# A hybrid diffusion layer on one core: another order for the prologue and for the gates of the mLSTM

## The chip, the cores and the metric

The kernel runs on one core of a Trainium2 chip. The metric is device time in microseconds (us), and a kernel's time is the median of its runs. The engines are TensorE (PE; PEld is its weight load), VectorE (DVE), ScalarE (ACT), GpSimd (POOL) and SyncE (SP). SP issues nearly all transfers, from one queue, in order.

## The reference

One layer over 1024 latent tokens and 256 context tokens, 1024 wide, float32. Cut to the steps that matter:

```
mod = silu(c) @ w_mod + b_mod                  # 6 pieces of 1024: shift, scale, gate, twice
p   = (LN(x) * (1 + scale1) + shift1) @ w_in   # the same for ctx, with silu(c_ctx)
i, f = p_gates[..., :8] + b, log_sigmoid(p_gates[..., 8:] + b)
mix = [HGRN2(p), mLSTM(conv3x3(q, k), v, i, f)]     # both scan forward and backward
x   = LN(alpha * x + gate1 * (readout(mix) @ w_out))
x   = LN(alpha * x + gate2 * PEER(LN(x) * (1 + scale2) + shift2))   # 8 heads, top 16 of 16384 experts
```

The mLSTM needs running sums of `f` and running maxima per chunk of 128 tokens, in both directions.

## The kernel before

A scheduler decides the order of the instructions on every engine when the kernel is built; the program's order is its guide, and an instruction marked `keep_in_program_order` is not moved ahead of what stands before it. Each engine then runs its own list in order, and waits where an input or a buffer isn't ready. A named tile with `bufs=n` is a ring of n buffers, handed out in the order of the program.

Four stages come before PEER.

**Prologue** (`modcols` L89, `inputs_ln` L164). The first 2048 columns of `w_mod` (shift and scale) come in 8 tiles `w` of 1 MB. For each, TensorE multiplies 1536 columns by the two conditioning vectors (L116), and VectorE sums the last 512 (`macc`, L120 and L122). Two context tiles are loaded ahead of them, `wf` (1 MB of `w_in`) amid them, and the eight tiles of x behind them (L159). The result is turned into columns `modc` (L133, L135). Then each group of tokens is normalised, transposed to PSUM, modulated by ScalarE into `xf` (L180), and split into a high half (float16, L181, VectorE) and a low half (bfloat16, L182, VectorE or, for two of eight k, GpSimd): `xmT`. All projections take both halves.

**Gates** (`gates` L237). 16 columns per token are projected (`oa`), transposed to rows of tokens on 64 partitions (L261), made into log sigmoids there (L266 to L270), scanned by VectorE (L280 to L325), and transposed back to columns `gcol` (L331). The columns are used in the mLSTM alone.

**HGRN2** (`hgrn` L342). Values are projected in two halves (`inputs`, L230, 240 matmuls each), then 8 rounds of `one`, whose projections are L222. `modrows` (L669) makes the other 4096 modulation columns meanwhile: 32 tiles `wm` of 512 KB in a ring of its own, two buffers deep, two matmuls each (L686). `Uprep` (L185) is spread through the stage: it loads one of 128 tiles of the expert table (`us`, 512 KB, ring of two in pool `up`), casts it to a high half (ScalarE, L198), subtracts for the low half (GpSimd, L199), and stores both (`Ud`, L202). 96 of the 128 are called before the mLSTM.

**mLSTM** (`mlstm` L508). For each half of q and k, projections go to a padded grid (`pad`, L545), and VectorE runs the 9 taps of the convolution (L553, L555) over 1024 elements per partition, and after it the chunk states. Readout, output projection and PEER follow.

Of the kernel before, what the change touches and what calls it, by code (L numbers as in the profile page):

```python
# [17 lines left out]
D = 1024  # L18
LAT = 1024
CTX = 256  # L20
# [68 lines left out]
def modcols(g, I, mp, lp):  # L89
# [16 lines left out]
    ps = [g.pp.tile([128, 512], F32, name=n, bufs=2 if n == "pj" else 1) for n in ("pj", "pj", "sc")]  # L106
    acc = mp.tile([128, 2, 512], F32, name="macc")
    xs = inputs_load(g, I, lp, 0, 2)
    g.w0 = []
    for k in range(KD):  # L110
        if k == KD // 2:
            g.w0.append(W(g, I, HI))
        wt = mp.tile([128, 2048], F32, name="w0", bufs=8)
        nc.sync.dma_start(wt, I["w_mod"][0, k * 128:(k + 1) * 128, 0:2048])
        for b in range(3):
            nc.tensor.matmul(ps[b][0:2], g.cs[:, k::8], wt[:, b * 512:(b + 1) * 512], start=(k == 0), stop=(k == KD - 1))  # L116
        for j in range(2):
            c = g.cs[:, 8 * j + k:8 * j + k + 1]
            if k == 0:
                nc.vector.tensor_scalar(acc[:, j], wt[:, 1536:], c, None, op0=OP.mult)  # L120
            else:
                nc.vector.scalar_tensor_tensor(acc[:, j], wt[:, 1536:], c, acc[:, j], op0=OP.mult, op1=OP.add)  # L122
    xs += inputs_load(g, I, lp, 2, NT)
    mr = mp.tile([128, 2048], F32, name="w0", bufs=8)[0:2]
    for b in range(3):
        (nc.scalar.copy if b % 2 else nc.vector.tensor_copy)(mr[:, b * 512:(b + 1) * 512], ps[b][0:2])
    pt = g.pp.tile([128, 512], F32, name="tr", bufs=2)
    for b in range(12, 16):
        for j in range(2):
            nc.tensor.matmul(pt[:, 2 * b + j:2 * b + j + 1], acc[:, j, (b - 12) * 128:(b - 11) * 128], g.ones, start=True, stop=True)  # L130
    for b in range(12):
        nc.tensor.transpose(pt[:, 2 * b:2 * b + 2], mr[:, b * 128:(b + 1) * 128], g.ident[0:2, 0:2])
    nc.vector.tensor_tensor(g.modc, pt[:, 0:32].rearrange("p (b j) -> p b j", j=2),  # L133
                            bT[:, :, None].to_broadcast([128, 16, 2]), op=OP.add)
# [29 lines left out]
def inputs_ln(g, xs, sp):  # L164

    nc = g.nc
    for t0, n in ((0, 2), (2, 4), (6, 4)):
# [4 lines left out]
        for k in range(KD):  # L172
# [8 lines left out]
            nc.vector.tensor_copy(g.xmT[0][:, k, sl], f)  # L181
# [55 lines left out]
def gates(g, I, w):  # L237
    nc, tc = g.nc, g.tc
    gp = g.gp
    with tc.tile_pool(name="gt", bufs=1, reuse_waits="tile") as tp:  # L240
        gb = tp.tile([128, 16], F32, name="gb")
        nc.sync.dma_start(gb, rowb(I["ml_gate_b"], 0, 16))
        ps = g.pp.tile([128, 512], F32, name="oa")
        for t in range(NT):
            proj_t(g, w, t, ps[:, t * 16:(t + 1) * 16])
        gt = tp.tile([128, NT, 2, 64], F32, name="gt")
        nc.vector.memset(gt, 0.0)
        psv = ps[:, :NT * 16].rearrange("p (t a d h) -> p t a d h", a=2, d=2, h=4)
        gbv = gb.rearrange("p (a d h) -> p a d h", a=2, d=2)
        for a in range(2):  # L250
            for d in range(2):
                nc.vector.tensor_tensor(gt[:, :, a, 32 * d:32 * d + 4], psv[:, :, a, d, :],
                                        gbv[:, None, a, d, :].to_broadcast([128, NT, 4]), op=OP.add)
        rows = []
        for a in range(2):
            r = tp.tile([64, SQ], F32, name=f"row{a}")
            for t0 in range(0, NT, 4):
                n = min(4, NT - t0)
                pt = g.pp.tile([128, 512], F32, name="sc")
                for i in range(n):  # L260
# [8 lines left out]
        lf = fr  # L269
        nc.vector.scalar_tensor_tensor(lf, fr, 0.0, e, op0=OP.min, op1=OP.subtract)  # L270
        one = tp.tile([64, NT, 128], F32, name="one")
        neg = tp.tile([64, NT, 128], F32, name="neg")
        nc.vector.memset(one, 1.0)
        nc.vector.memset(neg, 0.0)
        nc.vector.memset(one[:, :, 0:1], 0.0)
        nc.vector.memset(neg[:, :, 0:1], -BIG)
        oneF, negF = (x.rearrange("p t s -> p (t s)") for x in (one, neg))
        a = tp.tile([64, NT, 128], F32, name="ga")
        aF = a.rearrange("p t s -> p (t s)")
        nc.vector.tensor_tensor_scan(aF[0:32], oneF[0:32], lf[0:32], 0.0, op0=OP.mult, op1=OP.add)  # L280
# [24 lines left out]
        nc.vector.tensor_copy(mp_[32:64, 2:NT - 1], mn[32:64, 3:NT])
        ml = tp.tile([64, NT], F32, name="gml")
# [1080 lines left out]
```

## Time and profile before

| | us |
|---|---|
| median of 3 runs (3216.59 to 3222.46) | 3220.53 |
| the profiled execution, its own time | 3223.63 |
| its span | 3221.9 |
| TensorE busy | 2938.5 |
| VectorE busy | 2611.8 |
| GpSimd busy | 1846.0 |
| ScalarE busy | 1181.8 |

The busy times are of the whole span, most of which is PEER; the change lies in the first 900 us. There a stage is read by which engine has no idle time in it, and by what the other engines wait for.

### The profile page before, as it was taken

The page shows a single profiled execution, that of the slowest core. Times are in us where ns is not written, and L with a number is a line of the kernel's source. Part 1 is how long each engine was busy: PE and PEld are TensorE (multiplying, and loading weights), DVE is VectorE, ACT ScalarE, POOL GpSimd, SP SyncE. Part 2 cuts the span into 40 slices and gives each one's busy share as a digit, 9 for nine tenths or more (in the row PEclk, how much of TensorE's full clock was granted, in tenths as well). Part 3 has the DMA queues.
Part 4 walks back from the last instruction along what each step waited for, and adds up shares of the span by engine and source line. Part 5 has one row for each costly group of instructions (what it writes and reads, how often), then busy time and mean ns, then how long its engine had stood idle before and what let it go on. Part 6 is the DMA issues. An engine that isn't in the chain of part 4 may idle for free.

```text
span 3221.9 us, 50811 instructions
## 1 busy us (share of the span) xinstructions
PE 2938.5 (91%) x18943; PEld 1892.4 (59%) x18943; DVE 2611.8 (81%) x5352; ACT 1181.8 (37%) x1699; POOL 1846.0 (57%) x1358
## 2 busy tenths in 40 slices
PE   7898989888898799799999989999999999999985
PEld 4644556657786567577777875555555555554432
DVE  8434464999878899888877777898999998988998
ACT  4465563324345532126666653222222222222111
POOL 3555675422347465416566665676666666666664
PEclk8899998898899899899999999999999999999987
DMA  7688666421267689758889998999999999999994
GB/s 282 213 289 291 213 207 232 139 64 55 103 221 268 210 324 331 288 176 279 300 278 297 307 345 324 355 368 364 359 364 360 360 354 366 355 347 336 342 327 183
DMA packets 319548, 900.33 MB, mean 279 GB/s; under 512 B 28076, under 2 KB 107572, under 8 KB 311364
## 3 DMA queue, kind: packets, MB, share of 16 engines
q1 hardware_dynamic: 208708, 494.38, 43.3%
q0 software_dynamic: 110592, 402.70, 34.2%
q8 instruction: 149, 2.44, 0.3%
q14 instruction: 99, 0.81, 0.1%
HBM read 758.67 MB, written 138.30 MB: 278 GB/s over the span
## 4 chain that ended last, share of the span: by engine, by line
PE 42%; DVE 24%; DMA 11%; POOL 9%; issue 9%; ACT 4%; SPq 0%; DVEq 0%; POOLq 0%; ACTq 0%
PE y L1164 16%; PE S L1131 12%; DMA row<-in_peer_v_dram,idx 5%; POOL row L1072 4%; DVE row L1091 3%; PE pj L222 3%; DVE mz L555 3%; PE pj L230 2%; DVE us L1034 2%; POOL vs L1147 2%; DMA us<-in_peer_ut_dram 2%; DMA row<-in_peer_u_dram,idx 2%; DVE hg L1099 2%; POOL uT L199 2%; PE y L1039 1%
## 5 line engine op out<-in xcount | busy, mean ns | idle before, releaser
L1164 PE MATMUL y<-vs,w 128*128 128x512 bf16 x3840 | 878.9, 382 | 40.5 <-POOL vs L1147 16.6
L1131 PE MATMUL S<-hTd,uT 128*128 128x320 f16 (+1 forms) x6144 | 898.6, 300 | 10.7 <-issue 6.2
L1131 PEld LDWEIGHTS <-uT 128*128 128x128 bf16 x6144 | 602.6, 98 | 276.0 <-issue 13.2
L1164 PEld LDWEIGHTS <-w 128*128 128x128 bf16 x3840 | 378.2, 98 | 471.4 <-issue 61.4
L1099 DVE SCALAR_TENSOR_TENSOR hg<-row,dot,hg 128x1024 f32<-128x1024 f32 x381 | 489.5, 1285 | 110.3 <-DMA row<-in_peer_v_dram,idx 94.7
L1072 POOL DMA_INDIRECT row<-in_peer_u_dram,idx x384 | 387.4, 1009 | 287.2 <-DVE row L1091 135.2
L1072 POOL DMA_INDIRECT row<-in_peer_v_dram,idx x384 | 387.4, 1009 | 219.7 <-DVE hg L1099 133.2
L1091 DVE SCALAR_TENSOR_TENSOR row<-row,hg 128x1024 f32<-128x1024 f32 x384 | 458.7, 1211 | 58.1 <-DMA row<-in_peer_u_dram,idx 52.1
L199 POOL TENSOR_TENSOR uT<-us,uT 128x1024 bf16<-128x1024 f32 x128 | 303.9, 2379 | 188.7 <-ACT uT L198 173.1
L1146 ACT CAST vs<-row 128x1024 bf16<-128x1024 f32 x128 | 133.5, 1043 | 488.7 <-DMA row<-in_peer_v_dram 467.0
L1147 POOL TENSOR_TENSOR vs<-row,vs 128x1024 bf16<-128x1024 f32 x128 | 277.9, 2171 | 28.7 <-ACT vs L1146 23.1
L1035 POOL TENSOR_TENSOR kT<-us,gf 128x512 f32<-128x512 bf16 x160 | 178.3, 1137 | 200.3 <-DVE us L1034 175.5
L222 PE MATMUL pj<-xmT,wb 128*128 128x512 f16 (+3 forms) x1248 | 262.5, 367 | 19.9 <-ACT pad L545 18.5
L1136 ACT ACTIVATE ge<-S 128x320 f32<-128x320 f32 x256 | 111.8, 441 | 408.2 <-PE S L1131 299.5
L230 PE MATMUL pj<-wb,xmT 128*128 128x256 f16 (+1 forms) x1728 | 224.3, 290 | 22.4 <-DVE rsg L748 12.0
L1171 DVE TENSOR_TENSOR ya<-ya,y 128x512 f32<-128x512 f32 x310 | 207.3, 681 | 26.1 <-PE y L1164 24.3
L230 PEld LDWEIGHTS <-xmT 128*128 128x128 f16 (+1 forms) x1968 | 186.6, 103 | 65.0 <-issue 24.1
L222 PEld LDWEIGHTS <-wb 128*128 128x128 f16 (+1 forms) x1248 | 123.8, 101 | 147.7 <-issue 43.3
L1040 ACT COPY gst<-y 128x512 f32<-128x512 f32 x160 | 171.3, 1075 | 83.9 <-PE y L1039 66.0
L1034 DVE TENSOR_TENSOR us<-iob,eT 128x512 bf16<-128x512 bf16 x320 | 172.4, 588 | 14.6 <-ACT kT L1036 9.0
L1039 PE MATMUL y<-kT 128*128 128x128 f32 x1280 | 165.2, 281 | 17.1 <-ACT kT L1036 8.1
L198 ACT CAST uT<-us 128x1024 bf16<-128x1024 f32 x128 | 133.2, 1044 | 122.9 <-DMA us<-in_peer_ut_dram 96.5
(390 smaller groups left out, 3927.8 us busy)
## 6 DMA issues: line engine op xcount, KB each, us to landing
us<-in_peer_ut_dram SPq DMA_DIRECT2D x128, 512.0 KB
Ud<-uT SPq DMA_DIRECT2D x128, 512.0 KB
uT<-Ud SPq DMA_DIRECT2D x128, 512.0 KB
row<-in_peer_v_dram SPq DMA_DIRECT2D x128, 512.0 KB
Gd<-gst SPq DMA_DIRECT2D x20, 1984.0 KB
Gt<-Gd SPq DMA_DIRECT2D x31, 1280.0 KB
Sd<-ge SPq DMA_DIRECT2D x66, 320.0 KB
kT<-Sd SPq DMA_DIRECT2D x66, 320.0 KB
```

The source lines that it names most:

```text
L199: nc.gpsimd.tensor_tensor(lo, uf, hi, op=OP.subtract)
L222: g.nc.tensor.matmul(ps[:, :t1 - t0], w.t[a][:, k, c0:c0 + 128], g.xmT[b][:, k, t0:t1], start=(k == 0 and a == b), stop=(k == KD - 1 and a ...
L230: g.nc.tensor.matmul(ps, g.xmT[a][:, k, t * 128:(t + 1) * 128], w.t[b][:, k, :w.n], start=(k == 0 and a == b), stop=(k == KD - 1 and a == 1))
L1034: nc.vector.tensor_tensor(cm[:, a], g.iob, eT[:, a, None, t0:t0 + 4].to_broadcast([128, 128, 4]), op=OP.is_equal)
L1039: nc.tensor.matmul(ps[:, i * 128:(i + 1) * 128], oh[:, 0, i], oh[:, 1, i], start=True, stop=True)
L1072: d = g.nc.gpsimd.indirect_dma_start(out=b, out_offset=None, in_=self.I["peer_u" if n < 128 else "peer_v"][0], in_offset=bass.IndirectOffs ...
L1091: nc.vector.scalar_tensor_tensor(b, b, 1.0, self.ps, op0=OP.mult, op1=OP.mult, accum_out=dot[:, j:j + 1])
L1099: nc.vector.scalar_tensor_tensor(self.ps, b, dot[:, j:j + 1], self.ps, op0=OP.mult, op1=OP.add)
L1131: m = nc.tensor.matmul(ps[:, :hn], uT[:, a, k, :], g.hTd[b][:, k, i * hn:(i + 1) * hn], start=(k == 0 and (a, b) == (0, 0)), stop=(k == KD ...
L1147: nc.gpsimd.tensor_tensor(v[:, 1], vf, v[:, 0], op=OP.subtract)
L1164: nc.tensor.matmul(ps, w[:, a, t * 128:(t + 1) * 128], v[:, b, h * 512:(h + 1) * 512], start=(n == 0), stop=(n == 3 * GI - 1))
L1171: nc.vector.tensor_add(ya, ya, ps)
```

## The change

1. All ten tiles of tokens are loaded ahead of `w_mod`, and `wf` behind it. All 2048 columns go through TensorE, as four blocks of 512 that land in four groups of 32 rows of one PSUM bank; VectorE's sums are gone. Four full transposes make the columns.
2. For odd k ScalarE writes the high half of `xmT` itself, from PSUM, instead of VectorE from `xf`.
3. The log sigmoid is taken before the transposes, with tokens on 128 partitions (80 elements in each), not after them with 1280. The transposes of rows alternate between two PSUM banks.
4. The transposes to `gcol` are a function `cols`, called behind both halves of the values' projections and their `Uprep` calls, and the first three of them are kept in program order. The pool of the gates stays open until then.
5. `modrows` loads its tiles into the ring `us`, which `Uprep` uses, and its own `wm` is gone.

```
 modcols:
-    acc = mp.tile([128, 2, 512], F32, name="macc")
-    xs = inputs_load(g, I, lp, 0, 2)
+    mr = mp.tile([128, 512], F32, name="mr")
+    nc.gpsimd.memset(mr, 0.0)
+    xs = inputs_load(g, I, lp, 0, NT)
     for k in range(KD):
-        if k == KD // 2:
-            g.w0.append(W(g, I, HI))
         wt = mp.tile([128, 2048], F32, name="w0", bufs=8)
         nc.sync.dma_start(wt, I["w_mod"][0, k * 128:(k + 1) * 128, 0:2048])
-        for b in range(3):
-            nc.tensor.matmul(ps[b][0:2], g.cs[:, k::8], wt[:, b * 512:(b + 1) * 512], ...)
-        for j in range(2):
...
-                nc.vector.scalar_tensor_tensor(acc[:, j], wt[:, 1536:], c, acc[:, j], op0=OP.mult, op1=OP.add)
-    xs += inputs_load(g, I, lp, 2, NT)
+        for q in range(4):
+            nc.tensor.matmul(ps[32 * q:32 * q + 2], g.cs[:, k::8], wt[:, q * 512:(q + 1) * 512], ...)
+    g.w0.append(W(g, I, HI))
+    for q in range(4):
+        o = slice(32 * q, 32 * q + 2)
+        (nc.scalar.copy if q % 2 else nc.vector.tensor_copy)(mr[o], ps[o])
...
+    for b in range(4):
+        nc.tensor.transpose(pt[:, b * 128:(b + 1) * 128], mr[:, b * 128:(b + 1) * 128], g.ident)
 inputs_ln:
-            nc.vector.tensor_copy(g.xmT[0][:, k, sl], f)
+            if k % 2:
+                nc.scalar.activation(g.xmT[0][:, k, sl], pt[:, :n * 128], AF.Identity, ...)
+            else:
+                nc.vector.tensor_copy(g.xmT[0][:, k, sl], f)
 gates:
+    f = tp.tile([128, NT, 2, 4], F32, name="gf")
+    e = tp.tile([128, NT, 2, 4], F32, name="gl")
+    nc.vector.tensor_tensor(f, psv[:, :, 1], gbv[:, None, 1].to_broadcast([128, NT, 2, 4]), op=OP.add)
+    nc.scalar.activation(e, f, AF.Abs)
+    nc.scalar.activation(e, e, AF.Exp, scale=-1.0)
+    nc.scalar.activation(e, e, AF.Ln, bias=1.0)
...
-                pt = g.pp.tile([128, 512], F32, name="sc")
+            pt = g.pp.tile([128, 512], F32, name=("sc", "up")[t0 // 4 % 2])
...
-        nc.scalar.activation(e, fr, AF.Abs)
-        nc.scalar.activation(e, e, AF.Exp, scale=-1.0)
-        nc.scalar.activation(e, e, AF.Ln, bias=1.0)
...
+    def cols():
         for t in range(NT):
             for i, s in enumerate((gq, ws, fl)):
-                nc.tensor.transpose(pt[:, i * 64:(i + 1) * 64], s[:, t, :], g.ident[0:64, 0:64])
+                mm = nc.tensor.transpose(pt[:, i * 64:(i + 1) * 64], s[:, t, :], g.ident[0:64, 0:64])
+                if t == 0:
+                    tc.keep_in_program_order(mm)
 hgrn:
-        gates(g, I, w1)
+        cols = gates(g, I, w1, gs.enter_context(tc.tile_pool(name="gt", bufs=1, reuse_waits="tile")))
...
         g.uprep(8)
         inputs(1)
         g.uprep(8)
+        cols()
+        gs.close()
 modrows:
-                wt = mp.tile([128, 1024], F32, name="wm", bufs=2)
+                wt = g.up.tile([128, 2, D], BF, name="us").rearrange("p a b -> p (a b)").bitcast(F32)
```

The order shows three places. SP's queue at the start of the program, before (`xt` are tokens, `w` is `w_mod`, `wf` a block of `w_in`, `us` a tile of the expert table):

```order
L159 DMA xt<-in_ctx_dram 128x1024 x2
L114 DMA w_143<-in_w_mod_dram 128x2048
L114 DMA w_150<-in_w_mod_dram 128x2048
L114 DMA w_157<-in_w_mod_dram 128x2048
L114 DMA w_164<-in_w_mod_dram 128x2048
L213 DMA wf<-in_w_in_dram 128x2048
L114 DMA w_177<-in_w_mod_dram 128x2048
L114 DMA w_184<-in_w_mod_dram 128x2048
L114 DMA w_191<-in_w_mod_dram 128x2048
L114 DMA w_198<-in_w_mod_dram 128x2048
L159 DMA xt<-in_x_dram 128x1024 x8
L195 DMA us<-in_peer_ut_dram 128x1024 x2
```

and in the changed kernel:

```order
L150 DMA xt<-in_ctx_dram 128x1024 x2
L150 DMA xt<-in_x_dram 128x1024 x8
L113 DMA w_158<-in_w_mod_dram 128x2048
L113 DMA w_164<-in_w_mod_dram 128x2048
L113 DMA w_170<-in_w_mod_dram 128x2048
L113 DMA w_176<-in_w_mod_dram 128x2048
L113 DMA w_182<-in_w_mod_dram 128x2048
L113 DMA w_188<-in_w_mod_dram 128x2048
L113 DMA w_194<-in_w_mod_dram 128x2048
L113 DMA w_200<-in_w_mod_dram 128x2048
L207 DMA wf<-in_w_in_dram 128x2048
L689 DMA us<-in_w_mod_dram 128x1024 x2
```

The tokens moved ahead of `w_mod`, `wf` behind it, and the first two `us` are tiles of `modrows`. All 32 tiles of `modrows` now stand in the queue ahead of the first load of the expert table.

TensorE amid the values' projections (`pj<-wb,xmT`), where the first transposes to `gcol` stand (`row`, `ge` and `ga` are the gates' rows), before:

```order
L230 MATMUL pj<-wb_1450,xmT_108 128x256
L230 LDWEIGHTS xmT_109
L230 MATMUL pj<-wb_1449,xmT_109 128x256
L331 MATMUL sc<-ident,row_833 128x64
L331 MATMUL up<-ident,row_833 128x64
L230 LDWEIGHTS xmT_108
L230 MATMUL pj<-wb_1449,xmT_108 128x256
```

and in the changed kernel, where the projections for HGRN2 (L216) begin behind them:

```order
L224 MATMUL pj<-wb_1363,xmT_109 128x256
L329 MATMUL sc<-ident,row_817 128x64
L329 MATMUL sc<-ident,ge 128x64
L329 MATMUL sc<-ident,ga 128x64
L329 MATMUL up<-ident,row_817 128x64
L329 MATMUL up<-ident,ge 128x64
L329 MATMUL up<-ident,ga 128x64
L216 LDWEIGHTS wb_1749
L216 MATMUL pj<-xmT_108,wb_1749 128x512
```

The transposes moved from the middle of the second half of the projections to its end.

ScalarE in the second part of the mLSTM, where `pad` is filled for the convolution, before:

```order
L545 COPY pad_4649<-pj 128x8x64
L557 ACT_TABLE_LOAD
L557 ACTIVATE mz_5877<-mz_5877,cwT 128x1024
L545 COPY pad_4647<-pj 128x8x64
L730 ACT_TABLE_LOAD
L730 ACTIVATE rrs_6461<-rrs_6461,eps 128x16
L620 ACT_TABLE_LOAD
L620 ACTIVATE dm<-dm 128x512
L545 COPY pad_4647<-pj 128x8x64
L560 COPY cpad<-pj 128x256
L568 ACT_TABLE_LOAD
L568 ACTIVATE mz_6009<-mz_6009,cwT 128x256
```

and in the changed kernel (L192 is the cast of `Uprep`, L198 before; L551, L563 and L574 are L545, L557 and L568 before):

```order
L551 COPY pad_4624<-pj 128x8x64
L192 CAST uT<-us 128x1024
L736 ACT_TABLE_LOAD
L736 ACTIVATE rrs_6438<-rrs_6438,eps 128x16
L626 ACT_TABLE_LOAD
L626 ACTIVATE dm<-dm 128x512
L551 COPY pad_4624<-pj 128x8x64
L192 CAST uT<-us 128x1024
L566 COPY cpad<-pj 128x256
L192 CAST uT<-us 128x1024 x3
L574 ACT_TABLE_LOAD
L574 ACTIVATE mz_5986<-mz_5986,cwT 128x256
```

Before, one cast of `Uprep` stands behind the fourth `pad` of the first half, and none in the rest of the mLSTM. Now 25 stand there. The tables before that place are short by as many: up to the first round of HGRN2 (the first L397) ScalarE has 25 casts in its list before, and 2 now.

## Rows read from the trace of the kernel before

**Rows 1.** Windows: stretch, length, busy of PE, PEld, DVE, ACT, POOL (instructions), granted clock, DMA share, GB/s.
```profile
30.00:84.00 54.00, 41.17 (x428) 30.57 (x427) 53.43 (x97) 27.33 (x46) 28.07 (x16) 0.75 0.65 235
```

**Rows 2.** Timeline, first 40 us: start, length, engine, line, work, idle before.
```profile
12.84 1.41 DVE L122 SCALAR_TENSOR_TENSOR macc<-w,cs,macc 128x512 f32<-128x512 f32 x2 [1.71 <-DMA w<-in_w_mod_dram]
20.22 1.90 ACT L76 CAST wb<-wf 128x2048 f16<-128x2048 f32 x1 [11.26 <-DMA wf<-in_w_in_dram]
30.28 1.41 DVE L122 SCALAR_TENSOR_TENSOR macc<-w,cs,macc 128x512 f32<-128x512 f32 x2 [0.16 <-DMA w<-in_w_mod_dram]
37.97 0.11 DVE L135 TENSOR_SCALAR modc<-modc 128x16 f32<-128x16 f32 x1
```

**Rows 3.** Timeline, layer norm and modulation of the tokens.
```profile
49.73 0.75 DVE L170 TENSOR_SCALAR xt<-xt,lnmv,lnrs 128x1024 f32<-128x1024 f32 x1
53.73 2.22 POOL L199 TENSOR_TENSOR uT<-us,uT 128x1024 bf16<-128x1024 f32 x1 [0.99 <-ACT uT L198]
53.88 2.62 DVE L170 TENSOR_SCALAR xt<-xt,lnmv,lnrs 128x1024 f32<-128x1024 f32 x1
62.49 0.77 ACT L180 ACTIVATE xf<-ob,modc 128x512 f32<-128x512 f32 x1
81.81 0.68 DVE L182 TENSOR_TENSOR xmT<-xf,xmT 128x512 bf16<-128x512 f32 x1
```

**Rows 4.** Groups of VectorE, 38 to 84 us: count, busy, mean ns, idle before.
```profile
L182 DVE TENSOR_TENSOR xmT<-xf,xmT 128x512 bf16<-128x512 f32 (+1 forms) x18 | 15.2, 866 | 0.1
L181 DVE CAST xmT<-xf 128x512 f16<-128x512 f32 (+1 forms) x24 | 12.4, 542 | 0.0
L170 DVE TENSOR_SCALAR xt<-xt,lnmv,lnrs 128x1024 f32<-128x1024 f32 x8 | 8.3, 1042 | 0.0
```

**Rows 5.** Timeline of TensorE around the gates' transposes.
```profile
93.14 3.11 PE L230 MATMUL pj<-wb,xmT 128*128 128x256 f16 x27
125.61 0.34 PE L331 MATMUL sc<-ident,row 64*128 64x64 f32 x1 [5.12 <-DVE row L284]
125.99 9.64 PE L230 MATMUL pj<-wb,xmT 128*128 128x256 f16 x72
142.03 0.36 PE L331 MATMUL sc<-ident,ge 64*128 64x64 f32 x1 [6.40 <-ACT ge L320]
142.43 4.70 PE L230 MATMUL pj<-wb,xmT 128*128 128x256 f16 x24
```

**Rows 6.** Chain in order of time, one tile of modrows: start, length.
```profile
171.62 0.96 PE tr L686 x4
```

**Rows 7.** Waits of TensorE, 200 to 555 us: total, times, longest.
```profile
PE tr L686 <- DMA wm<-in_w_mod_dram: 8.4, 5, 3.7
```

**Rows 8.** Windows of the low-half subtraction, line L199.
```profile
43.00:196.00 153.00, 58.44 (x25) 0.86 0.66 232
553.00:606.00 53.00, 24.64 (x9) 0.90 0.60 213
606.00:755.00 149.00, 0.00 (x0) 0.90 0.21 66
```

**Rows 9.** Windows of VectorE, all its work, second part of mLSTM.
```profile
606.00:755.00 149.00, 136.62 (x288) 0.90 0.21 66
```

**Rows 10.** Windows of the convolution's taps, line L555.
```profile
553.00:606.00 53.00, 42.36 (x22) 0.90 0.60 213
606.00:755.00 149.00, 63.41 (x42) 0.90 0.21 66
```

**Rows 11.** Tile mz, one tap: ns least, median, most.
```profile
L555 DVE SCALAR_TENSOR_TENSOR mz<-pad,cwT,mz x64: 1253/1276/5087, 555.7 to 751.9; 128x1024 f32<-128x1024 f32 x64
```

**Rows 12.** Timeline of table loads and their casts.
```profile
351.44 0.38 SPq L195 DMA_DIRECT2D us<-in_peer_ut_dram  x1
356.98 1.04 ACT L198 CAST uT<-us 128x1024 bf16<-128x1024 f32 x1 [6.18 <-DMA us<-in_peer_ut_dram]
360.68 0.38 SPq L195 DMA_DIRECT2D us<-in_peer_ut_dram  x1
```

More of the change, by code (lines that the diff above doesn't have):

```diff
@@ new lines, in gates @@
+    gb = tp.tile([128, 16], F32, name="gb")
+    nc.sync.dma_start(gb, rowb(I["ml_gate_b"], 0, 16))
+    ps = g.pp.tile([128, 512], F32, name="oa")
+    for t in range(NT):
+        proj_t(g, w, t, ps[:, t * 16:(t + 1) * 16])
+    gt = tp.tile([128, NT, 2, 64], F32, name="gt")
+    nc.vector.memset(gt, 0.0)
+    psv = ps[:, :NT * 16].rearrange("p (t a d h) -> p t a d h", a=2, d=2, h=4)
+    gbv = gb.rearrange("p (a d h) -> p a d h", a=2, d=2)
+    f = tp.tile([128, NT, 2, 4], F32, name="gf")
+    e = tp.tile([128, NT, 2, 4], F32, name="gl")
@@ new lines, in gates @@
+    rows = []
+    for a in range(2):
+        r = tp.tile([64, SQ], F32, name=f"row{a}")
+        for t0 in range(0, NT, 4):
+            n = min(4, NT - t0)
+            pt = g.pp.tile([128, 512], F32, name=("sc", "up")[t0 // 4 % 2])
+            for i in range(n):
+                nc.tensor.transpose(pt[0:64, i * 128:(i + 1) * 128], gt[:, t0 + i, a, :], g.ident)
+            nc.vector.tensor_copy(r[:, t0 * 128:(t0 + n) * 128], pt[0:64, :n * 128])
+        rows.append(r)
+    ir, fr = rows
+    e = tp.tile([64, SQ], F32, name="ge")
@@ new lines, in gates @@
+    lf = fr
+    one = tp.tile([64, NT, 128], F32, name="one")
+    neg = tp.tile([64, NT, 128], F32, name="neg")
+    nc.vector.memset(one, 1.0)
+    nc.vector.memset(neg, 0.0)
+    nc.vector.memset(one[:, :, 0:1], 0.0)
+    nc.vector.memset(neg[:, :, 0:1], -BIG)
+    oneF, negF = (x.rearrange("p t s -> p (t s)") for x in (one, neg))
+    a = tp.tile([64, NT, 128], F32, name="ga")
+    aF = a.rearrange("p t s -> p (t s)")
+    nc.vector.tensor_tensor_scan(aF[0:32], oneF[0:32], lf[0:32], 0.0, op0=OP.mult, op1=OP.add)
@@ L327, in gates @@
+    nc.sync.dma_start(g.win, win)
+    ws = e.rearrange("p (t s) -> p t s", s=128)
+    nc.vector.tensor_tensor(ws, gq, ml[:, :, None].to_broadcast([64, NT, 128]), op=OP.subtract)
+    nc.scalar.activation(ws, ws, AF.Exp)
+    cd = tp.tile([64, NT], F32, name="gcd")
+    nc.vector.tensor_sub(cd, mp_, ml)
+    nc.scalar.activation(cd, cd, AF.Exp)
+    fl = a
+    nc.vector.tensor_add(fl, a, M)
+    nc.scalar.activation(fl, fl, AF.Exp, scale=-1.0)
+    def cols():
         g.col = gp.tile([128, NT, 3, 2, 4], F32, name="gcol")
@@ L339, in gates @@
         nc.vector.tensor_copy(g.cd, pb[:, :8 * NT].rearrange("p (r t) -> p r t", t=NT))
+    return cols
 def hgrn(g, I, w0, w1):
```

151 lines of the change are left out of this document (50 added, 101 removed).

## The prediction

> **What bounds the kernel now.** I read the windows by engine first, to see in which stretch an engine has no idle time, then the timeline where a stage ends, then the waits there, and last the windows of single lines where the change puts work.
>
> Up to 30 us the transfers set the pace. Seven tiles of 1 MB of `w_mod` and `wf` land between the sums at 12.84 and at 30.28 [rows 2], which is 2.49 us for 1 MB, and each of these sums waits for its tile. The columns `modc` are there at 38.1. From 30 to 84 us VectorE is the bound: 53.43 busy of 54.00, while TensorE has 41.17 [rows 1]. The last write of `xmT` ends at 81.81 + 0.68 = 82.5 [rows 3]. Then TensorE projects values and stops twice for transposes to `gcol`: 5.12 us for the scan, 6.40 for ScalarE behind it [rows 5]. In HGRN2 it waits little for `modrows`, 8.4 us in 5 waits [rows 7]. From 606 to 755, the second part of the mLSTM, VectorE is the bound again, 136.62 of 149.00 [rows 9], and no table subtraction of GpSimd runs there; 25 run between 43 and 196, and 9 between 553 and 606 [rows 8].
>
> So the change touches four stages with three bounds. A saving counts only where the engine that it helps is the last one, and what it moves may land where VectorE has nothing to spare.
>
> **modc: 5.4 us later.** Eight tiles of x (4 MB) go ahead of `w_mod`, and `wf` (1 MB) behind it: 3 MB more, 7.5 us, so the last tile of `w_mod` lands at about 37.8 instead of 30.3, and `wf` at 40.2. ScalarE copies two of the four blocks `mr`, and its order has the first cast of `wf` between them, which takes 1.90 [rows 2]: it can start at 40.2, so the second copy ends at about 42.7, and four transposes and the additions bring `modc` to 43.5. The removed sums of VectorE (1.41 each) lay beside the transfers and give nothing.
>
> **xmT: done 12 us sooner.** From 38.1 to 82.5 VectorE had 44.4 us of work without a gap. What no longer stands behind `modc`: the normalisation, 8.3 in eight L170 [rows 4], since x is there before the last `w_mod`; and 12 of 24 casts L181 at 542 ns, 6.5, now ScalarE's. That leaves 29.6. The table's subtractions go out of the stretch too, since the first loads of `us` are `modrows`'. L182 takes 866 ns in the mean beside them [rows 4] and 0.68 by itself [rows 3], so its 18 give back 3.3, and 26.3 are left. ScalarE gets 12 more passes of about 0.77 [rows 3], 24 + 12 of them, 27.7 at most: the two are level. So 43.5 + 27 = 70.5, 12 us sooner. Bounds: 8.7 if L182 does not get faster, 15 if the statistics that stood there go as well.
>
> **The stalls at the gates: 14.7 us.** `cols` stands behind both halves' projections, and its inputs are by then long done: before, the last was there at 142.0 with half of the projections still to come. Both stalls go, 5.12 + 6.40 = 11.5. After each stall projections ran slower: 72 in 9.64 and 24 in 4.70, where 27 took 3.11 in the undisturbed stretch [rows 5], so 72 would have taken 8.3 and 24 2.8; 3.2 more. Bounds: 11.5 (what was slow stays so) and 14.7, of which I take the upper. The log sigmoid by columns is hidden in both forms once nothing waits for `gcol`.
>
> **modrows: 2 us.** The 32 tiles are 32 x 0.96 = 31 us of TensorE [rows 6]; 26 of them move from HGRN2 ahead of it. TensorE pays them here instead of there: nothing, apart from the waits. The 8.4 of [rows 7] go. In the ring of two `us` a load lands 5.5 us after its issue (351.44, with the cast at 356.98) and the next is issued 9.2 after the first [rows 12], while TensorE's order has 43 matmuls of the values between two tiles and the next two: 43 x 3.11 / 27 = 4.95 [rows 5], and 1.92 for the tiles themselves, 6.9. So some tiles will be late. Bounds: 8 gained if they fill gaps of TensorE in the stage to 84 us, where it is idle for 12.8, and 12 lost. I take 8.4 - 6.4 = 2 gained.
>
> So the stages up to HGRN2 end 12 + 14.7 + 2 = 28.7 us sooner (bounds: 8 and 38). As HGRN2 is TensorE's nearly throughout, this is handed on.
>
> **The table's preparations: 19 us lost.** `modrows` takes the places of loads at the start, so `Uprep` runs later: ScalarE's list has 25 casts ahead of the first round of HGRN2 before, and 2 now, and 25 stand in the mLSTM where there was 1. What do 24 more subtractions on GpSimd cost VectorE, which is the bound there? Three rows bear on it. Beside a subtraction of 2.22, one L170 took 2.62 instead of 0.75 [rows 3]: the whole wait. Between 553 and 606, 22 taps took 42.36 [rows 10] and at the median of 1276 [rows 11] would have taken 28.1: 14.3 for 9 subtractions, 1.6 each (a little less, as other work of GpSimd was there). From 606 on the taps are 63.41 of VectorE's 136.62 [rows 9, 10]; if only they are held up, that is 1.6 x 0.46 = 0.74. VectorE's other work there may be held up as L170 was, so I take 1.2 each, between the two: 24 x 1.2 = 29. VectorE's idle time of 12.4 takes up some 10 of it, so 19 is lost. Bounds: 24 x 0.74 - 12 = 6 below, and above, each subtraction at its full length, 58.44 / 25 = 2.34 [rows 8]: 56 - 12 = 44.
>
> The Trainium skill bears on this place ("SBUF — State Buffer", "SBUF: two separate sides" and "Who interferes with whom"): VectorE and GpSimd share a pair of ports under an exclusive lock, a VectorE instruction with two SBUF inputs contends with a GpSimd one that reads SBUF, and the later one waits for the whole instruction. The 2.62 of [rows 3] agrees; the 1.6 per subtraction of [rows 10, 11] is less than a whole one. By the rule at its hardest the outcome is the first rival's.
>
> **The sum.** -28.7 + 19 = -9.7 against the profiled execution's own 3223.63: 3213.9. The median of the runs is 3.1 lower: 3210.8, **3211**. Its own range is 3200 to 3227. PEER follows unchanged and is handed the difference whole.
>
> **Rivals.**
>
> *Slower: VectorE is held for the whole subtraction.* Place: 606 to 755. Price: 44 instead of 19, so 3220.5 - 28.7 + 44 = 3236. It decides from 1.6 us per preparation on, where 24 x 1.6 less 10 of idle time eats the 28.7. For it: L170 at 2.62 [rows 3], and the 1.6 of the taps stands just at that point. Against it: half of VectorE's time there isn't taps, and TensorE and ScalarE set parts of the stretch.
>
> *The preparations fit into gaps.* The 6 of the lower bound: 3220.5 - 28.7 + 6 = 3198. For it: ScalarE's casts and GpSimd's start come one by one, with time between, and VectorE has 12.4 idle. Against it: the 42.36 of [rows 10].
>
> *The change does not deliver: `modrows` waits for its loads.* If a pair of tiles takes 9.2 as in [rows 12], and TensorE's list holds 6.9 of work for it, 16 pairs lose 2.3 each, 37 us, and the early gain is gone: 3220.5 - 28.7 + 37 + 19 = 3248. For it: both users share two buffers, and TensorE cannot pass a late tile. Against it: before, the same tiles in two buffers cost 8.4 [rows 7], and a buffer of `modrows` is free after TensorE's two matmuls, one of `Uprep` only after a cast and a subtraction.
>
> **Chances.** My forecast 0.45, whole subtractions 0.27, gaps 0.20, loads 0.08. A measurement of this kernel tells a difference from about 0.2%, 6.4 us: faster is below 3214, slower above 3227. Of my case 0.25 is faster, 0.17 within, 0.03 slower; whole subtractions give 0.08 within and 0.19 slower; gaps 0.18 faster and 0.02 within; loads 0.08 slower. Faster 0.43, same 0.27, slower 0.30. The range goes from 3194, below the case of gaps, to 3238, above that of whole subtractions; past it lie the late loads and both bounds together.
>
> **What would show it.** In the profile of the changed kernel: `modc` at about 43.5 and the last write of `xmT` at about 70.5; no stall of 5 us at the transposes to `gcol`; TensorE's waits for `us` tiles of `w_mod` summing to some 6 us, not 30; the first round of HGRN2 some 25 us further on in the work than before at the same time. From 600 to 760, about 24 subtractions where there were none, and taps at a mean above their 1.51 (63.41 / 42) of before; VectorE's busy time there some 29 up, without more work. If the taps' mean stays at 1.5, the gaps were enough; if it goes to 2.3 or more, the first rival holds. I am wrong altogether if `xmT` is not sooner, if TensorE stalls elsewhere for the gates, or if VectorE is not the bound between 600 and 760.

## The result: 0.2 to 0.5% slower

The changed kernel took 3241.74 us in the median of 7 runs, and the kernel before 3222.46 on the same chip: a ratio of 1.0054, interval 1.0034 to 1.0074. On a second chip, with 12 runs, it was 1.0022 (1.0011 to 1.0034). Forecast were 3211 and a range to 3238. The profiled execution has a span of 3235.2 us, 13.3 more than before.

### The profile page after: what moved, and what is told of

Read it like the earlier page. It is cut to its first block, busy times and chain, and to the rows that moved or that the text cites. A ratio compares the mean times of both kernels' runs of the same rounds, so it can differ in the third digit from the quotient of the medians.

```text
span 3235.2 us, 50764 instructions
## 1 busy us (share of the span) xinstructions
PE 2931.2 (91%) x18935; PEld 1888.5 (58%) x18935; DVE 2604.6 (81%) x5324; ACT 1184.8 (37%) x1714; POOL 1840.4 (57%) x1359
## 4 chain that ended last, share of the span: by engine, by line
PE 30%; DVE 17%; DMA 9%; issue 6%; POOL 6%; ACT 1%; another core or an unknown queue 1%; DVEq 0%; SPq 0%; POOLq 0%; ACTq 0%
PE y L1170 13%; PE S L1137 12%; DMA row<-in_peer_v_dram,idx 5%; DVE hg L1105 3%; DVE row L1097 3%; POOL row L1078 3%; PE y L1045 2%; POOL vs L1153 2%; DVE us L1040 2%; DMA row<-in_peer_u_dram,idx 1%; DMA us<-in_peer_ut_dram 1%; DVE alt L884 1%; DVE ya L1177 1%; PE S L916 1%
## 5 line engine op out<-in xcount | busy, mean ns | idle before, releaser
L1137 PEld LDWEIGHTS <-uT 128*128 128x128 bf16 x6144 | 604.5, 99 | 295.0 <-issue 28.7
L193 POOL TENSOR_TENSOR uT<-us,uT 128x1024 bf16<-128x1024 f32 x128 | 303.0, 2374 | 204.8 <-ACT uT L192 184.7
L216 PE MATMUL pj<-xmT,wb 128*128 128x512 f16 (+3 forms) x1248 | 266.8, 371 | 12.9 <-ACT pad L551 9.7
L216 PEld LDWEIGHTS <-wb 128*128 128x128 f16 (+1 forms) x1248 | 125.6, 103 | 141.0 <-issue 36.0
L1040 DVE TENSOR_TENSOR us<-iob,eT 128x512 bf16<-128x512 bf16 x320 | 165.8, 566 | 28.3 <-ACT kT L1042 20.1
L192 ACT CAST uT<-us 128x1024 bf16<-128x1024 f32 x128 | 133.0, 1044 | 138.2 <-DMA us<-in_peer_ut_dram 115.4
L77 POOL TENSOR_TENSOR wb<-wf,wb 128x2048 bf16<-128x2048 f32 (+1 forms) x19 | 78.1, 4113 | 174.1 <-ACT wb L76 137.7
```

What stands on the lines that cost most here:

```text
L193: nc.gpsimd.tensor_tensor(lo, uf, hi, op=OP.subtract)
L216: g.nc.tensor.matmul(ps[:, :t1 - t0], w.t[a][:, k, c0:c0 + 128], g.xmT[b][:, k, t0:t1], start=(k == 0 and a == b), stop=(k == KD - 1 and a ...
L1040: nc.vector.tensor_tensor(cm[:, a], g.iob, eT[:, a, None, t0:t0 + 4].to_broadcast([128, 128, 4]), op=OP.is_equal)
L1137: m = nc.tensor.matmul(ps[:, :hn], uT[:, a, k, :], g.hTd[b][:, k, i * hn:(i + 1) * hn], start=(k == 0 and (a, b) == (0, 0)), stop=(k == KD ...
```

## The profile after

The timeline of the changed kernel, where the columns are made and where `xmT` ends:

```profile
43.31 0.58 ACT L119 COPY mr<-pj 2x512 f32<-2x512 f32 x1
43.37 4.06 POOL L77 TENSOR_TENSOR wb<-wf,wb 128x2048 bf16<-128x2048 f32 x1 [41.82 <-ACT wb L76]
45.38 2.08 DVE L126 TENSOR_SCALAR modc<-modc 128x16 f32<-128x16 f32 x1
...
70.85 1.29 DVE L176 TENSOR_TENSOR xmT<-xf,xmT 128x512 bf16<-128x512 f32 x2
```

`modc` is there at 47.5, and `xmT` at 72.1 (before 82.5 [rows 3]). TensorE behind it:

```profile
119.97 0.59 PE L224 MATMUL pj<-wb,xmT 128*128 128x256 f16 x2 [3.37 <-ACT hv L382]
...
151.39 4.06 PE L216 MATMUL pj<-xmT,wb 128*128 128x512 f16 x18
```

The stalls at the transposes [rows 5] are gone, and one of 3.37 stands at the values' projections, for ScalarE's copy `hv`. ScalarE makes this copy behind the gates' `ge`, and `ge` came late. VectorE's L315, which makes its input, took 5.35 us beside GpSimd's split L77 of a block of weights; the same operation (L319) took 1.48 before. First before, then after:

```profile
137.86 1.48 DVE L319 TENSOR_TENSOR ge<-row,gml 64x1280 f32<-64x1280 f32 x1
```

```profile
111.52 5.39 POOL L77 TENSOR_TENSOR wb<-wf,wb 128x2048 bf16<-128x2048 f32 x1 [25.34 <-ACT wb L76]
112.91 5.35 DVE L315 TENSOR_TENSOR ge<-row,gml 64x1280 f32<-64x1280 f32 x1
118.29 1.27 ACT L316 ACTIVATE ge<-ge 64x1280 f32<-64x1280 f32 x1 [5.54 <-DVE ge L315]
```

The first projection of HGRN2 (`pj<-xmT,wb`) is at 151.39. Before it was at 146.97, but now 20 of 32 tiles of `modrows` are done by then. In the second part of the mLSTM, windows of VectorE, of GpSimd's line L193 (L199 before), and of the taps (L561, L555 before):

```profile
603.00:780.00 177.00, 164.04 (x280) 0.84 0.58 195
603.00:780.00 177.00, 57.02 (x24) 0.84 0.58 195
603.00:780.00 177.00, 73.29 (x41) 0.84 0.58 195
```

Against [rows 8 to 10]: 24 subtractions where there were none, and VectorE busy 164.04 of 177 where it was 136.62 of 149, with no work added. Its idle time is 13.0, and was 12.4. The two windows are not cut alike, though: that of before ends 3 us behind the last tap. From the 23rd to the last tap, first before, then after, VectorE is busy 31.3 us more, and idle 13.0 instead of 12.0:

```profile
606.00:751.90 145.90, 133.88 (x281) 0.90 0.22 67
602.10:780.20 178.10, 165.14 (x282) 0.84 0.58 196
```

The groups of VectorE in that part show who pays; first before, then after:

```profile
L555 DVE SCALAR_TENSOR_TENSOR mz<-pad,cwT,mz 128x1024 f32<-128x1024 f32 x42 | 63.4, 1521 | 0.1
L621 DVE TENSOR_TENSOR dm<-dm,qk 128x512 f32<-128x512 f32 x10 | 10.7, 1070 | 1.7 <-ACT qk L585 1.3 <-ACT dm L620 0.4
L638 DVE TENSOR_TENSOR dn<-dn,gcol 128x2 f32<-128x2 f32 x16 | 5.7, 353 | 0.1
```

```profile
L561 DVE SCALAR_TENSOR_TENSOR mz<-pad,cwT,mz 128x1024 f32<-128x1024 f32 x42 | 75.5, 1815 | 0.1
L627 DVE TENSOR_TENSOR dm<-dm,qk 128x512 f32<-128x512 f32 x10 | 15.0, 1499 | 3.1 <-ACT qk L591 2.0 <-ACT dm L626 1.1
L644 DVE TENSOR_TENSOR dn<-dn,gcol 128x2 f32<-128x2 f32 x16 | 11.9, 747 | 0.1
```

The 42 taps cost 12.1 us more, ten multiplications 4.3, and sixteen operations of 2 elements 6.2: 0.29 to 0.43 us more for each in the mean, whatever its length.

## The experiments

Each trace is read at six places: the end of the last write of `xmT`, the first projection of HGRN2 on TensorE, the first, 23rd and last tap of the mLSTM (between the last two lies its second part), and the first `idx` of PEER on VectorE. The last column is the ratio of the times to those of before on the same chip. All but the ratio are starts or ends of instructions in one trace, in us. Two traces of one kernel agree here within 2.2 us.

| kernel | xmT | HGRN2 | tap 1 | tap 23 | last tap | idx | ratio (interval) |
|---|---|---|---|---|---|---|---|
| before | 82.5 | 147.0 | 555.7 | 606.0 | 751.9 | 1129.9 | |
| before_again | 82.8 | 147.3 | 555.2 | 605.6 | 750.3 | 1129.2 | |
| changed | 72.1 | 151.4 | 551.7 | 602.1 | 780.2 | 1149.0 | 1.0054 (1.0034 to 1.0074) |
| after_again | 72.5 | 150.3 | 549.6 | 599.9 | 779.2 | 1150.4 | 1.0022 (1.0011 to 1.0034) |
| own_ring (1 to 4) | 84.6 | 159.4 | 551.7 | 602.0 | 750.2 | 1140.2 | 1.0005 (0.9984 to 1.0025) |
| ring_only (5) | 71.3 | 147.2 | 543.6 | 594.1 | 769.8 | 1146.1 | 0.9998 (0.9980 to 1.0016) |
| gates_only (3, 4) | 82.0 | 156.6 | 548.2 | 598.6 | 746.2 | 1124.7 | 1.0001 (0.9986 to 1.0016) |
| ring_gates (3 to 5) | 70.9 | 149.0 | 548.7 | 599.2 | 776.9 | 1146.8 | 1.0044 (1.0027 to 1.0061) |
| prologue_only (1, 2) | 84.3 | 150.1 | 554.2 | 602.6 | 747.4 | 1124.2 | 0.9976 (0.9961 to 0.9991) |
| no_read | 72.9 | 152.4 | 538.9 | 589.2 | 741.4 | 1111.6 | 0.9949 (0.9930 to 0.9967) |
| late_table | 71.6 | 151.0 | 547.5 | 597.9 | 742.8 | 1123.2 | 1.0063 (1.0044 to 1.0081) |
| ring_late | 70.9 | 146.9 | 541.8 | 590.2 | 735.7 | 1120.4 | 1.0056 (1.0039 to 1.0074) |
| short_after | 72.0 | 142.0 | 519.5 | 569.9 | 749.6 | 1121.4 | 0.9942 (0.9926 to 0.9958) |
| short_before | 82.7 | 147.2 | 558.2 | 605.2 | 749.9 | 1129.6 | 1.0007 (0.9993 to 1.0021) |
| quiet | 70.7 | 136.0 | 557.6 | 608.0 | 757.9 | 1136.4 | 1.0036 (1.0021 to 1.0052) |
| quiet_prologue | 72.7 | 142.2 | 552.7 | 603.1 | 752.7 | 1131.1 | 1.0031 (1.0014 to 1.0049) |
| quiet_gates | 71.2 | 147.8 | 544.5 | 594.8 | 750.7 | 1128.0 | 0.9967 (0.9950 to 0.9983) |

The runs were on several chips, whose medians of before go from 3208 to 3225; spans of different chips are not compared.

**The two kernels again.**

> The kernel before itself, for a trace from the same chip as the others. If executions agree up to PEER, its milestones to 1100 us lie within 3 us of the first trace of it; if chips or executions differ there, by up to 12 us in HGRN2, the differences of the other traces have to be taken against this one.

> The changed kernel itself, timed on the chip of the experiments. If the loss is its own: ratio 1.003 to 1.007 again, and some 30 us lost in the second part of the mLSTM, as in its first trace. If it was an accident of one chip: a ratio within 0.2% of 1.

Up to PEER, before agrees with its first trace within 1.6 us: the places may be compared across chips. The loss of the change is its own: its second ratio, 1.0022, is below the 1.003 to 1.007 that were expected, but its interval excludes 1, and the second part of the mLSTM takes 179.3 us instead of 144.7 in before_again.

**One part undone, and parts alone.** The theory then was that `modrows` had left gaps that hid it, and that the subtractions hold VectorE; its rival, that parts 1 to 4 bring nothing.

```
 own_ring, on the changed kernel:
-                wt = g.up.tile([128, 2, D], BF, name="us").rearrange(...).bitcast(F32)
+                wt = mp.tile([128, 1024], F32, name="wm", bufs=2)
```

> The changed kernel with the tiles of modrows back in a ring of their own (part 5 undone, parts 1 to 4 kept). Theory A (part 5 is what costs: the matmuls of modrows leave the gaps of HGRN2, where they were nearly free, and the table's subtractions land on VectorE's bound stretch of the mLSTM): the 17 us of the change turn into a gain of 10 to 20 against before, about 3205, first round of HGRN2 some 10 us sooner than before, taps at a mean of about 1.5 us in the second part of the mLSTM. Theory B (parts 1 to 4 bring nothing, since TensorE's work behind xmT is the bound): 3222 or more, no faster than before.

It was the rival's number, 1.0005, but not its reason: `xmT` itself is there at 84.6, no sooner than before. The mLSTM's second part (602.0 to 750.2) is nearly as short as before, as the theory had it.

ring_only is the opposite edit on the kernel before.

> The kernel before with part 5 alone: modrows loads into the ring us. Theory A: slower by 25 to 40 us, about 3255, with the second part of the mLSTM some 28 longer and the rest lost in the input stage and HGRN2. Theory B: within 8 us of before.

Theory B's number at the end, 0.9998, but far from unmoved on the way. `xmT` is 11.2 us sooner with no other part in; 21 tiles of `modrows` stand ahead of HGRN2, which begins when it did before; the mLSTM begins 12.1 us sooner; and its second part takes 175.7 instead of 145.9, which is what theory A had for it.

gates_only takes `gates` and `hgrn` of the changed kernel into the one before.

> The kernel before with parts 3 and 4 alone (log sigmoid by columns, transposes to gcol behind the projections). Theory A: the two stalls of 5.1 and 6.4 us go, 10 to 15 us faster, about 3210. Theory B: the stalls go, but another wait takes their place in HGRN2, within 5 us of before.

The rival's number, for a plainer reason: a stall is still there. HGRN2 begins 9.6 us later, with 10 tiles of `modrows` (9.6 us of TensorE) ahead of it. The waits of TensorE between 75 and 205 tell why:

```profile
PE up L335 <- ACT ge L322: 7.9, 1, 7.9
PE sc L267 <- DVE neg L278: 3.2, 1, 3.2
```

11.1 us again, for the same chain: ScalarE's `ge` and VectorE's work ahead of it. L335 are the transposes to `gcol` (L331 before). Part 4 keeps only the first three of them in program order; here the scheduler moved three others, which go to `up`, amid the projections, and the stall is at the second of them:

```profile
121.87 0.27 PE L335 MATMUL up<-ident,row 64*128 64x64 f32 x1
130.05 0.37 PE L335 MATMUL up<-ident,ge 64*128 64x64 f32 x1 [7.91 <-ACT ge L322]
```

So parts 3 and 4 alone don't take this stall away; in the changed kernel all of these transposes stand at the end.

prologue_only takes `modcols` and `inputs_ln` of the changed kernel into the one before.

> The kernel before with parts 1 and 2 alone (tokens first, all columns on TensorE, odd high halves by ScalarE). Forecast of the prediction: xmT 12 us sooner and handed on, ratio 0.996. Rival (TensorE's projections behind xmT are the bound then): xmT is 10 us sooner, the first round of HGRN2 no more than 4, ratio 0.999 to 1.

Neither was right on `xmT`, which was 1.8 us later. Its last write shows it:

```profile
81.09 3.23 DVE L176 TENSOR_TENSOR xmT<-xf,xmT 128x512 bf16<-128x512 f32 x2
```

Yet the kernel is 0.24% faster than before, the first version that beats both; the places show some 5 us of it up to PEER, most of it gained behind 550. What makes that is open.

ring_gates has all but the prologue.

> The kernel before with parts 3, 4 and 5 (gates and ring, not the prologue). It tells which of parts 1 to 4 brings the first round of HGRN2 from 198.8 us with part 5 alone to 206 in the changed kernel. If the prologue (modc at 47 instead of 38): some 199 here. If the gates' new place: some 205.

By the mark that these numbers are of, ScalarE's first logarithm in HGRN2 (L397 before), the first round is at 205.3 here, against 198.8 in ring_only and 206.3 in the changed kernel: the gates' new place brings most of it, as the second side had it. Earlier marks split it more evenly: the first sigmoid is at 188.4, against 185.2 and 192.4, and the first projection at 149.0, against 147.2 and 151.4.

**The table's subtractions in the mLSTM.**

```
 no_read, on the changed kernel:
+            if 72 <= self.n < 96:
+                nc.gpsimd.memset(lo, 0.0)
+            else:
                 nc.gpsimd.tensor_tensor(lo, uf, hi, op=OP.subtract)
 late_table, on the changed kernel (ring_late: on ring_only), in three places:
-    g.uprep(1)
+    g.uprep(g.uprep.n < 72)
```

> The changed kernel, in which 24 of the table's 128 subtractions (tiles 72 to 95, those that run in the second part of the mLSTM) are a memset of the low half by GpSimd: the low half of these tiles is left out, their loads, casts and stores stay. Theory A (GpSimd's subtraction, which reads two tiles, holds VectorE's instructions up): VectorE's busy time between 603 and 780 falls by about 27, taps back from 1.8 to 1.5 us in the mean, the kernel 25 us shorter, about 3216. Rival (the casts of ScalarE, the loads and stores, or the clock make that part longer): no more than 5 us shorter, taps still at 1.8.

> The changed kernel, whose HGRN2 and mLSTM prepare 72 tiles of the expert table and not 96; the 24 others follow where the last 32 already are, between 900 and 1100. Theory A (the 24 subtractions hold VectorE up between 603 and 780, and that is most of the loss): no loss of 30 us there, up to 860 about 15 us sooner than before; the end depends on whether the stretch from 900 to 1100, where VectorE is busy 85 of 100, takes 24 more: 3200 or less (0.997 or better) if it takes them at half price, no gain against the changed kernel if they cost the same 30 us there.

> The kernel before with part 5 alone, and 72 tiles prepared ahead of PEER as in the run above. In the trace of part 5 alone xmT was ready 11 us sooner and at 374 us it was 24 us ahead, all of it lost again up to 760. If the 24 subtractions are the cause: still some 10 to 20 us ahead at 860, and the best of all, ratio 0.994 to 0.997. If something else in the mLSTM takes it: no better than 0.999.

VectorE in the second part, in no_read, and in late_table:

```profile
590.00:743.00 153.00, 137.01 (x296) 0.91 0.66 226
```

```profile
598.00:745.00 147.00, 135.83 (x285) 0.90 0.20 66
```

In both it is busy 136 to 137 as before, with casts, loads and stores of the table in place in the first and gone in the second. late_table keeps its lead of 7 to 9 us through the mLSTM, and ring_late one of 14 to 16, as its expectation had it. It is GpSimd's subtraction that costs, and theory A holds here; a memset in its place, which only writes and takes 0.95 us, does not:

```profile
L194 POOL MEMSET uT<- x23: 947/951/953, 593.2 to 686.8; 128x1024 bf16 x23
```

The 24 tiles can't be had for nothing later, though. In late_table TensorE stands still from 1121.7 to 1183.1, at the start of PEER, for a cast of query weights (L76) that stands behind the late table's casts in ScalarE's order. ring_late has the same wait of 61.4, and both kernels end 0.6% slower than before; that ring_late would be the best of all was wrong.

```profile
PE S L916 <- ACT uT L76: 61.4, 1, 61.4
```

One caution: up to its first tap no_read's engines have the same lists as the changed kernel's, and from its first projection to the first tap it still takes 386.5 us, where the changed kernel takes 400.3 and 399.3. In that stage some 14 us between single traces prove little alone. TensorE in this stretch, in the changed kernel and in no_read:

```profile
151.40:551.70 400.30, 362.54 (x2067) 0.88 0.60 205
152.40:538.90 386.50, 348.32 (x2042) 0.92 0.62 212
```

With the same list it is busy 14.2 us less, at a granted clock of 0.92 instead of 0.88 (25 fewer of its matmuls have a record in the second trace), and its idle time is as long. The second trace of the changed kernel and late_table have 0.88 too. Why no_read was granted more is open.

**What modrows costs TensorE, in either place.**

```
 short_after and short_before:
+                    n = 512 if k == 0 else 2
-                    nc.tensor.matmul(ps[32 * q:32 * q + 1], ..., wt[:, i * 512:(i + 1) * 512], ...)
+                    nc.tensor.matmul(ps[32 * q:32 * q + 1, 0:n], ..., wt[:, i * 512:i * 512 + n], ...)
```

> The changed kernel, in which 30 of 32 tiles of modrows are multiplied in 2 columns of 512 instead of all (most of these modulation columns is left out; all loads stay). It tells what TensorE's 31 us for modrows cost in their new place. If they are on the path there: the first round of HGRN2 18 to 22 us sooner and the kernel 20 to 27 us faster than the changed one. If they fill gaps: no more than 8.

> The kernel before, in which 30 of 32 tiles of modrows are multiplied in 2 columns of 512 instead of all (most of these modulation columns is left out; all loads stay): what TensorE's 31 us for modrows cost in their old place. The same edit made the changed kernel 26 us shorter. If they are on the path in HGRN2 too: about 25 us shorter, ratio 0.992. If they lie in gaps there: under 10.

The tiles of k = 0 keep all their columns, so 28 of the 32 tiles are short, and not 30 as the expectations say. The same edit gives 0.8%, 23.6 us, in the changed kernel (1.0022 to 0.9942, on one chip): they are on its path. It gives nothing in the one before. The places of short_after do not say where the time lies: HGRN2 begins 8.3 us sooner than in after_again and then takes 21.8 less, with only 12 of the tiles in it, and single traces of that stage differ by 14.

Windows of all engines from 197 to 380, before (its second trace), and short_before:

```profile
197.00:380.00 183.00, 167.14 (x929) 84.81 (x927) 87.83 (x120) 98.45 (x114) 114.84 (x51) 0.95 0.75 263
```

```profile
197.00:380.00 183.00, 153.51 (x910) 89.27 (x909) 84.77 (x120) 92.57 (x108) 116.78 (x51) 0.86 0.76 267
```

The same windows of the line of `modrows`' matmuls alone (L686, L687):

```profile
197.00:380.00 183.00, 27.36 (x104) 2.32 (x104) 0.95 0.75 263
```

```profile
197.00:380.00 183.00, 7.91 (x104) 2.40 (x104) 0.86 0.76 267
```

These matmuls take 19.5 us less, and TensorE is busy only 13.6 less, at a granted clock of 0.86 instead of 0.95, a mean between its two levels of 1.2 and 2.4 GHz: what is left took 5.8 more. The other 13.6 became idle time, and the stage ends no sooner. The waits for the tiles rose:

```profile
PE tr L686 <- DMA wm<-in_w_mod_dram: 8.1, 5, 3.8
```

```profile
PE tr L687 <- DMA wm<-in_w_mod_dram: 13.9, 4, 7.7
```

**Is a lead at HGRN2's start worth anything?** What was open by then: whether the table's subtractions beside `xmT` hold it up, and whether 11 us there reach the end.

```
 quiet (on before), quiet_prologue (on prologue_only), quiet_gates (on gates_only), in hgrn ahead of gates:
         v = vp.tile([128, NT, 512], F32, name="hv")
+        g.uprep(2, True)
```

> The kernel before with one line more: two of the table's tiles are called ahead of the gates, the first cast kept in program order, so that no subtraction of the table runs beside xmT (5 of them run later, 2 in the second part of the mLSTM). If the subtractions are what part 5 takes out of the way: xmT at 71 to 73 without any part of the change. If that lead is handed on (TensorE has no modrows to do there): first projection of HGRN2 at 136 to 140, and 5 to 10 us at the end, ratio 0.997 to 0.9985. If TensorE's work behind xmT or the gates' chain holds it: first projection at 145 or later, ratio 0.999 to 1.001.

> The same line in the kernel with parts 1 and 2 alone. xmT at 72 if modc at 47 is still the start of 25 us. If parts 1 and 2 free VectorE for more than the later modc costs: first projection some 3 us sooner than in the run above. Otherwise some 3 later, as without the line (150.1 against 147.3).

> The same line in the kernel with parts 3 and 4 alone. With those parts alone TensorE did 10 tiles of modrows ahead of HGRN2 and waited 7.9 + 3.2 us for the gates all the same. If those waits came from the table's casts and subtractions standing in the gates' way: waits under 4 us and the first projection 8 us or more sooner than 156.6 beyond the 11 of xmT. If from the gates' chain itself: waits of 8 or more again.

quiet answers both. Without any part of the change `xmT` is there at 70.7 and HGRN2 begins at 136.0, 11.3 sooner than in before_again: handed on. And at the first tap, after 421.6 us of HGRN2 where it was 407.9, it is 2.4 us behind. Neither side of its expectation has that: the lead is lost in the stage that was taken to hand it on, and the kernel is 0.36% slower. TensorE in this stretch, in before_again and in quiet:

```profile
147.30:555.20 407.90, 373.78 (x2150) 0.92 0.71 247
136.00:557.60 421.60, 382.32 (x2149) 0.90 0.72 250
```

Of the 13.7 us more, 8.5 are busy time at a lower granted clock, and 5.2 idle time. The edit also moves five of the table's preparations into HGRN2 (76 subtractions there instead of 71), and what they cost there was not separated. The two other pairs say the same: against the same kernels without the line, HGRN2 begins 7.9 sooner in quiet_prologue and 8.8 in quiet_gates, and the first tap is 1.5 and 3.7 sooner. In quiet, TensorE's wait for tiles of `modrows` from 190 on is longer than in before:

```profile
PE tr L687 <- DMA wm<-in_w_mod_dram: 12.5, 3, 6.1
```

It was 8.1 in the row of before_again above. quiet_prologue has `xmT` at 72.7, as expected, 2 us later than quiet, and begins HGRN2 6.2 later, where 3 were expected in its worse case. quiet_gates has one wait of 12.0 for `ge`, again at a transpose to `gcol` amid the projections, so it is the gates' chain itself; at 0.33% under before it has the lowest ratio of the kernels that leave nothing out, though its interval overlaps that of prologue_only.

## Why the prediction was wrong, by its own steps

The forecast was 28.7 sooner at the end of HGRN2 and 19 lost behind it. In the trace it is 4.0 sooner at the first tap and 28.3 later at the last. Nearly 25 were missing ahead, and 13 behind. Three steps failed above all: that HGRN2 hands a lead on, that `modrows` costs nothing in its new place, and that VectorE's idle time takes up part of the subtractions' price.

**modc**: forecast 43.5, measured 47.5. The last tile came as forecast (TensorE takes it up at 38.05) and the second copy `mr` ended at 43.9 (42.7). Of the rest, 0.7 are the transposes and the first addition, and 2.0 the addition L126, 0.11 before [rows 2] and 2.08 now: it ended at 47.46, with GpSimd's split L77, which ran from 43.37 to 47.43.

**xmT**: forecast 70.5, measured 72.1; right in size, wrong in what makes it. Parts 1 and 2 alone bring it 1.8 later, ring_only and quiet 11 to 12 sooner. Taking the subtractions out of the stretch was priced at 3.3, with 8.7 left as a bound for the rest; it is the whole of it. With none of them there, `modc` to `xmT` takes 33.1 in quiet and in ring_only and 24.7 in the changed kernel: parts 1 and 2 save 8.4 there, where 14.8 (8.3 and 6.5) were forecast, and the later `modc` takes 9.4. That the sum came out near 70.5 is luck. The window of these subtractions up to the last write, before:

```profile
38.00:82.50 44.50, 15.79 (x7) 0.70 0.58 199
```

Seven, and from `modc` to `xmT` it takes 33.1 us in quiet, where none is left, instead of 44.4: 1.6 for each, as the taps had shown [rows 10, 11]. The forecast let them hold up only L182, and VectorE's other work beside them was held up too.

**The stalls**: forecast 14.7 gained. In the changed kernel they are gone from the transposes, as forecast, and the chain they stood for is not: 3.4 at the copies of `hv` there, 11.1 and 15.7 in gates_only and quiet_gates. With part 5 in, parts 3 and 4 had little to gain: in ring_only `modrows` fills the wait, of which 1.8 is left. The prediction priced the subtractions of the table alone; the split L77 of the weights is a subtraction of GpSimd too, and it cost 2.0 at `modc` and, through L315, the 3.4 here.

TensorE from `xmT` to HGRN2, before, then after, and after for the line of `modrows` alone (L692):

```profile
82.50:147.00 64.50, 52.93 (x488) 0.87 0.59 205
```

```profile
72.10:151.40 79.30, 75.93 (x608) 0.96 0.51 162
72.10:151.40 79.30, 22.91 (x80) 1.92 (x80) 0.96 0.51 162
```

Without the 20 tiles TensorE is busy 53.0 there, as before: the 3.2 of faster projections did not come. And the tiles took 1.15 each, not 0.96 [rows 6].

**modrows**: the step "TensorE pays them here instead of there: nothing" failed. In the changed kernel the tiles cost some 24 us (short_after), in the one before nothing (short_before). The forecast waits of 6.4 us, for which the prediction shows no working, did not come: 0.9 in the second trace. The rival of late loads fell too.

**Handed on**: "As HGRN2 is TensorE's nearly throughout, this is handed on" failed. quiet brings 11.3 us to its start and none to its end; short_before takes 22.8 of matmuls out of it and it ends no sooner. TensorE is busy 167 of 183 there, but that share is no bound: with less to do it ran at a lower clock and waited more. What does set the end, the granted clock, loads for tiles, or the chain of VectorE and ScalarE in a round, was not separated.

The sum of these: HGRN2 began 4.4 later, where the forecast would have it 7.5 sooner (12 + 14.7, less 20 tiles of 0.96), and it took 8.4 less, where 21.2 were forecast (-28.7 + 7.5). The 11.9 that were missing at its start are 1.6 of `xmT`, the wait of 3.4, the 3.2 of the projections and 3.7 of the longer tiles. Of the 12.8 missing in it, the clock is the likeliest part: in the first trace before, TensorE is busy 373.84 of 408.7 us at 0.92, and the changed kernel's 362.54, at 0.88, is 11.3 less, not the 19.2 of 20 tiles. no_read, with the same list at 0.92, took 386.5, 22.2 less than before.

**The table**: 24 preparations, right. VectorE's busy time between the two taps rose by 31.3, forecast 29. But "idle time takes up some 10" failed: 12.0 became 13.0. That idle time is waits for TensorE, ScalarE and GpSimd, the longest of 3.0 before; why none of it took up the added work was not tested. So the part lost 32.2 us (178.1 against 145.9) and not 19. The rival of whole subtractions (44) was about as near in effect, and not in mechanism: a preparation took 1.30 of VectorE, where 1.2 was forecast and 2.34 was the rival's price. The Trainium skill ("SBUF — State Buffer", "Who interferes with whom") has the rival's rule, and adds that a VectorE instruction with two SBUF inputs contends with a GpSimd instruction that reads SBUF and not with one that only writes it; the memsets of no_read, 137.01 busy in place of 164.04, agree.

**PEER "unchanged"**: of 28.3 at the last tap, 19.1 are left at the first `idx`, and 7 to 17 at the end, by the two ratios. In the two traces of one chip VectorE's wait for gathered rows between 1150 and 1800 is shorter in the changed kernel:

```profile
DVE hg L1099 <- DMA row<-in_peer_v_dram,idx: 52.5, 40, 3.3
```

```profile
DVE hg L1105 <- DMA row<-in_peer_v_dram,idx: 42.4, 36, 3.5
```

Whether that is the later start, the slightly different order, or chance between executions is not settled; in other kernels (late_table and ring_late, with their wait behind `idx`, aside), what is left of a lead or a loss at `idx` differs from the ratio by up to 17 us. The four traces with part 5 and its subtractions in the mLSTM (changed, after_again, ring_only, ring_gates) are 16 to 21 us late at `idx`, and their ratios go from 0.9998 (ring_only) to 1.0054. So the loss in the mLSTM is shown, and how much of it reaches the end is not explained.

## What to carry to other kernels

A busy share of 90% is no proof that an engine sets a stage's end; the test is a run in which it gets less to do, or an earlier start, read with the granted clock beside it. When two edits fill or remove the same wait, count it once. And work that is moved out of a crowded stretch has to be priced where it lands: here it bought 11 us beside `xmT` and cost 32 in the mLSTM.

## What the runs showed of the hardware

VectorE's short instructions lost as much beside GpSimd's subtractions as long ones: 16 operations of 2 elements went from 353 to 747 ns in the mean, and an addition of 16 elements took 2.08 us instead of 0.11, to the end of the GpSimd instruction beside it. 23 memsets of GpSimd in the places of 24 subtractions left VectorE's busy time where it was without them: 137.01 us of 153, and 135.83 of 147 in late_table, which has no work of the table there.

TensorE's time for a stage is not set by its list alone. The same list of HGRN2 took 400.3 us at a mean granted clock of 0.88 and 386.5 at 0.92. And where 19.5 us of its matmuls were left out of a stretch of 183, the clock was 0.86 instead of 0.95, what was left took 5.8 us more, and the kernel was no faster.
